# Where the matmuls' operands lie in on-chip memory: activations and split weights first, in a two-layer transformer trunk

## The chip, the cores and the metric

One core of a Trainium2 chip runs the whole program in one launch. The metric is the device time of one execution in microseconds (us); lower is better. Three executions of the kernel before took 2267.03 to 2269.26 us, with a median of 2267.74 us.

## What is computed

The input x has 256 tokens of 2048 float32 features. Two layers follow, with all products in float32 accuracy:

```python
# layer 0
hn = rmsnorm(h, attn_norm_g[0])
h  = h + diff_attention(hn, w_qkv, ...) @ w_o_a        # 8 heads, two softmax maps each, T5 bias
h  = h + square(relu(rmsnorm(h, mlp_norm_g[0]) @ w_in[0])) @ w_out[0]     # 2048 -> 8192 -> 2048
# shared keys, values, forget gates from rmsnorm(h, kv_norm_g): w_k, w_v, w_f
# layer 1
h  = h + forgetting_attention(rmsnorm(h, attn_norm_g[1]) @ w_q, k, v, c) @ w_o_b    # 16 heads
h  = h + square(relu(rmsnorm(h, mlp_norm_g[1]) @ w_in[1])) @ w_out[1]
out = rmsnorm(h, final_norm_g)
```

All weight matrices together are about 400 MB, and each number of them is read from DRAM once.

## The kernel before, in words

**The stream of weights.** Every weight matrix is cut into granules of 128 partitions x 1024 float32 numbers (512 KB). `load` (L161) brings one into a tile `raw` (4 buffers) from SyncE's DMA queue. `split` (L169, the copy in L171 on ScalarE) writes its high part `whi` in the matmul's rounded format float32r, and `split_low` (L173, L174 on VectorE) writes the remainder `wlo` = raw - whi. Both have 5 buffers, and up to 4 granules are split ahead of the products. Activations are held in the same manner: a tile of 128 x 2 x 512 numbers holds, for two blocks of 128 features, the high parts of 256 tokens and then their low parts. A product of float32 accuracy is then hi.hi + hi.lo + lo.hi.

**Two forms of unit.** TensorE holds one operand, the stationary one of 128 x 128, and streams the other, the moving one, through it.

- A token-major unit (kind B, `mm_b`, L185 to L187) makes 256 tokens x 512 columns. The *activation* is stationary, and the split *weights* move, 512 columns at a time: 3 matmuls for each of 2 token blocks and 16 row blocks, 96 in a unit of 2048 rows.
- A feature-major unit (kind A, `mm_a`, L200 and L203) makes 256 features x 256 tokens. The *weights* are stationary, and the activation moves: 512 columns (high and low parts) with whi in L200, and 256 columns with wlo in L203, 32 of each in a unit.

**Which activation tiles a unit reads.** Tiles `x0` to `x7` hold the normed residual stream (for the attention's and the MLP's first products and the shared keys and values). Tiles `hx0` to `hx7` hold the MLP's hidden activations, eight at a time, in layer 0 before that the attention's outputs, and in layer 1 the query operand. The four tiles `oT` hold the attention's outputs of layer 1. So:

| product | form | stationary | moving | units |
|---|---|---|---|---|
| values of both layers | B | x | whi, wlo | 8 |
| w_o_a | B | hx | whi, wlo | 4 |
| w_out of both MLPs | B | hx | whi, wlo | 32 |
| w_o_b | B | oT | whi, wlo | 12, of 24 or 48 matmuls, 384 in all |
| queries and keys of layer 0, keys of layer 1, w_in of both MLPs | A | whi, wlo | x | 88 |
| queries of layer 1 | A | whi, wlo | hx | 8 |

**The order of the work.** It is written out by hand: a list of slots, one granule of one unit each, and tables `pre`, `mid` and `post` that place the side work (softmax, norms, transposes, evacuations of results) before, amid and after a slot. Nothing is reordered by a scheduler.

**Where a tile lies.** All tiles in on-chip memory come from one pool. A tag takes its place in a partition when its first tile is made, behind the tags that came before it, with all its buffers, in steps of 32 bytes. The places in the kernel before, in bytes from the start of a partition:

| tiles | bytes each | before, from | to | after, from | to |
|---|---|---|---|---|---|
| x0 to x7 | 4096 | 38592 | 71360 | 1152 | 33920 |
| hx0 to hx7 | 4096 | 177568 | 210336 | 33920 | 66688 |
| oT x4 (hT too) | 4096 | 210336 | 226720 | 66688 | 83072 |
| whi x5 | 4096 | 89792 | 110272 | 83072 | 103552 |
| wlo x5 | 4096 | 110272 | 130752 | 103552 | 124032 |
| ident, tri, upto, h0 to h3, z1, zs, ssb, osb, wfs, gains | 384 to 4096 | 1152 | 38592 | 124032 | 161472 |
| raw x4, junk | 4096, 2048 | 71360 | 89792 | 161472 | 179904 |
| e, v, T/NC/gf, R, q, k, aT and small ones | up to 8192 | 130752 | 177568 | 179904 | 226720 |

Of the kernel before, what the change touches and what calls it, by code (L numbers as in the profile page):

```python
# [12 lines left out]
F32R = mybir.dt.float32r  # L13
# [5 lines left out]
DRAM = bass.MemoryType.DRAM  # L19

P = 128
D = 2048
S = 256
HD = 128
FF = 8192
NA = 8          # differential heads
NF = 16         # forgetting heads
CW = 512        # columns of a token-major unit
NCH = D // CW
# [4 lines left out]
SCALE = HD ** -0.5  # L34
NREL = 383      # rel = -255 .. 127

LA = 4          # granules split ahead of the products
NRAW = 4        # granules in flight from DRAM
NSPL = LA + 1


@with_exitstack
def kernel(ctx: ExitStack, tc: tile.TileContext, *args):
# [10 lines left out]

    # ------------------------------------------------------------------ constants
    ident = sb.tile([P, P], F32, tag="ident", name="ident")
# [7 lines left out]

    # 1 where a token is up to another: within a block of 128, and a block before
    upto = sb.tile([P, S], F32, tag="upto", name="upto")
# [4 lines left out]

    # residual stream, token-major, by chunks of 512 features
    h = [sb.tile([P, 2, CW], F32, tag=f"h{c}", name=f"h{c}") for c in range(NCH)]

# [3 lines left out]

    # the activation engine's tables come in beside the first loads
    warm = sb.tile([P, 1], F32, tag="warm", name="warm")  # L80
    nc.vector.memset(warm, 0.0)
    nc.scalar.activation(out=warm, in_=warm, func=AF.Exp)
    # gains as columns: rows of 128 features, transposed
    grow = [sb.tile([n, P], F32, tag="z1", bufs=2, name="grow") for n in (32, 50)]
# [36 lines left out]

    # ------------------------------------------------------------------ the stream of weights
    # side work by slot of the tensor engine: before its weights' split, amid it, and after the products
    pre, mid, post = (defaultdict(list) for _ in range(3))
    order = []      # (unit, granule, token tiles): what the tensor engine does

    class Gran:
        """Weights of one transfer: kk tiles of 128 rows, 1024 numbers a partition."""

# [3 lines left out]
    class Unit:  # L133
        """One result in two banks: its granules, its operand, and what takes it."""

# [9 lines left out]
    def unit_b(W, r0, nk, c0, xs, done):  # L145
        """[256, 512] = x . W[r0 : r0 + nk * 128, c0 : c0 + 512], token-major."""
        gs = []
        for k in range(0, nk, 2):
            src = W[r0 + k * P:r0 + (k + 2) * P, c0:c0 + CW].rearrange("(k p) c -> p k c", p=P)
            gs.append(Gran(src, 2))  # L150
        return Unit("B", gs, xs, done)

    def unit_a(W, c0, xs, done):
        """[256 features, 256 tokens] = (x . W[:, c0 : c0 + 256]) transposed."""
        gs = []
        for k in range(0, 16, 4):
            src = W[k * P:(k + 4) * P, c0:c0 + 256].rearrange("(k p) c -> p k c", p=P)
            gs.append(Gran(src, 4))
        return Unit("A", gs, xs, done)
# [51 lines left out]

    # ------------------------------------------------------------------ pieces
    def new_x(tag):
        """Two 128-row tiles of an operand: high parts of 256 tokens, then low parts."""
        return sb.tile([P, 2, 2 * S], F32R, tag=tag, name=tag)

    def turn(c, tps):
        """h[c] feature-major, into two banks."""
        for b in range(2):
            for j in range(2):  # L220
                for m in range(2):
                    f = (2 * b + j) * P
                    nc.tensor.transpose(tps[b][:, (j * 2 + m) * P:(j * 2 + m + 1) * P],  # L223
                                        h[c][:, m, f:f + P], ident)

    def split_turned(c, tps, gain, dst, bs=(0, 1)):
        """High and low parts of gain . h[c] turned, from two pieces of 512 columns."""
        at = [(b, j, 4 * c + 2 * b + j) for b in bs for j in range(2)]
# [17 lines left out]
    def rsqrt(ssum, n, scale, eps, name, bufs=1):  # L246
        """(ssum * scale + eps) ** -0.5 by columns: three Newton steps from the exponent's half."""
        v = sb.tile([P, n], F32, tag="rs_v", bufs=2, name="rs_v")
# [18 lines left out]
    class Norm:  # L267
        """Row statistics of the residual stream: rstd by token, and along the free axis."""

# [32 lines left out]
    def pair_sum(u):  # L302
        """The two halves of a feature-major unit's banks added: [128, 2, 256]."""
        z1 = sb.tile([P, 2, S], F32, tag="z1", bufs=2, name="z1")
# [14 lines left out]

    # ------------------------------------------------------------------ prologue: x, T5 bias, lambda  # L320
    XT = {}
# [16 lines left out]
    def bias_in():  # L338
        T = sb.tile([P, NA, S], F32, tag="tnc", bufs=2, name="T")
        # T[q, head, j] = F[head, q, 127 - q + j]: rows of 383, read 382 apart  # L340
        src = bias["F"].rearrange("h q r -> h (q r)")[:, 127:127 + P * (NREL - 1)]
# [5 lines left out]
    def build_lambda():  # L347
# [6 lines left out]
        nl = sb.tile([P, 1], F32, tag="nlam", name="nlam")  # L354
        # -(e1 - e2 + init)
        nc.vector.tensor_tensor(out=nl, in0=ex[:, 1:2], in1=ex[:, 0:1], op=ALU.subtract)
        nc.vector.tensor_scalar(out=nl, in0=nl, scalar1=-LAMBDA_INIT, scalar2=None, op0=ALU.add)
        bias["nlam"] = nl

    # ------------------------------------------------------------------ layer 0: differential attention  # L360
    vt = {}
# [139 lines left out]

    # boundary after the last product that a chunk of h takes
    def h_done(c, norm, gain, key, with_scale=False):
# [33 lines left out]

    n_mlp0, n_att1, n_mlp1 = (Norm.__new__(Norm) for _ in range(3))      # started by their first chunk

# [8 lines left out]
    def wo(W, kind, p0, p1, dones):  # L548
        """h += o . W over the head pairs p0 to p1; the last pair of the first two chunks comes last."""
        us = [unit_b(W[0], p0 * S, 2 * (p1 - p0), c * CW,  # L550
# [11 lines left out]

    # ------------------------------------------------------------------ squared-ReLU MLP
    HX = {}

    def mlp(l, norm, key, last, start=None):
        for q in range(4):
# [20 lines left out]
            for c in range(NCH):  # L588
                u = unit_b(w_out[l], q * D, 16, c * CW, lambda hk=hk: HX[hk], adds[c] if q < 3 else last[c])
                if l == 1 and q == 3 and c == NCH - 1:  # L590
                    # the last result: one token tile ends before the other
                    u.apart = True
# [6 lines left out]

    # ------------------------------------------------------------------ layer 1: forgetting attention  # L600
    fg = {}

    def gates(s0):
# [24 lines left out]
        def gate1():  # L628
            # z = logits by token; n = min(z, 0); t = exp(-|z|)
            zc = sb.tile([P, 2, 2 * NF], F32, tag="fg_zc", name="fg_zc")  # L630
# [14 lines left out]
        def gate2():  # L645
            # log1p(t) = 2 atanh(s), s = t / (2 + t) in [0, 1/3]
            t = fg["t"]
# [19 lines left out]
        def gate4():  # L667
            # log sigmoid = min(z, 0) - log1p(exp(-|z|))
            p = fg["p"]
# [5 lines left out]
        def sums():  # L675
            # over the tokens up to each: by head and token
            t = ps.tile([P, 512], F32, tag="sc", name="cs")
# [40 lines left out]
    def spread_c(g):  # L718
        """-c over the keys on every partition, causal on the diagonal blocks: diagonal 0 | full | diagonal 1."""
        t = sb.tile([P, 4, 3 * P], F32, tag="tnc", bufs=2, name="NC")  # L720
# [8 lines left out]
    def fox_pair(g, i):  # L729
        """Heads 4 g + 2 i and the next."""  # L730
        st = {}
# [87 lines left out]
    def v_first(s0):  # L819
        """Beside the first unit of layer 1: the forget gates, and the query operand."""  # L820
        gates(s0 + 4)
        xq_plan(s0)
# [10 lines left out]
    def qkv_f(g):  # L833
# [6 lines left out]
        for i in range(2):  # L840
# [3 lines left out]
            def then(e, plan=plan, i=i):  # L844
                # the last values come after the last queries
                plan(e, e + 7 if g < 3 else e + 17 - 7 * i)
# [14 lines left out]

    # ------------------------------------------------------------------ last MLP and the final norm
    fin = {}
# [43 lines left out]

    # ------------------------------------------------------------------ emission
    grs, at = [], []        # the granules as they come; how many the slots so far have taken
    for u, i, ms in order:  # L910
# [20 lines left out]
    load_x(2)  # L931
    # the tensor engine's clock comes up while the first rows are on their way
    busy = sb.tile([P, CW], F32, tag="junk", name="busy")
# [41 lines left out]
    for s in range(n + 2):  # L975
        for f in pre.pop(s, []):
            f()
        # while x comes in, one granule less is split ahead
        upto_g = min(ng, at[s] + (LA if s >= 8 else LA - 1)) if s < n else ng
# [31 lines left out]
def bucket_onehot():  # L1011
    """Row b, column r: 1 where the T5 bucket of rel = r - 255 is b."""
    rel = np.arange(-255, NREL - 255)
# [29 lines left out]
```

## Time and profile before

| | |
|---|---|
| median of three executions | 2267.74 us (2267.03 to 2269.26) |
| span of the profiled execution, first to last instruction | 2266.5 us |
| what lies around that span in the timed executions, median less span | 1.2 us |
| instructions | 28986 |
| TensorE, matmuls busy | 2234.6 us, 99% of the span |
| TensorE, weight loads busy (beside the matmuls) | 1874.0 us, 83% |
| VectorE busy | 1356.8 us, 60% |
| ScalarE busy | 1022.4 us, 45% |
| DMA | 416.06 MB, mean 184 GB/s |

How to read it: consecutive matmuls overlap in time, since each one's record reaches from its start to the modelled end of its pipeline. So "99% busy" says that TensorE hardly ever waits; it doesn't say how much time a matmul costs. What a matmul costs is the distance from its start to the start of the next one, called its step below, and it is read from a stretch of known length in which a known number of matmuls start.

### The profile page before, as it was taken

The numbers are of one execution on the slowest core, as the hardware profiler recorded it, in microseconds if no ns is written. First come the engines' busy times: TensorE is split into PE (matmuls) and PEld (weight loads), VectorE is DVE, ScalarE is ACT, GpSimd is POOL, SyncE is SP. The second block draws the span as 40 slices with busy tenths as digits, with TensorE's granted clock in tenths as the row PEclk, the third lists the DMA queues.
The fourth block names the chain that finished last, engine by engine and source line by source line (L and its number), as shares of the span: only waits on it lengthen the run. The fifth ranks groups of instructions, "written<-read, shape, count | busy, mean of one in ns | idle before, by whom it ended". The sixth has DMA issues, their size and how long they took to land.

```text
span 2266.5 us, 28986 instructions
## 1 busy us (share of the span) xinstructions
PE 2234.6 (99%) x11272; PEld 1874.0 (83%) x11272; DVE 1356.8 (60%) x1768; ACT 1022.4 (45%) x1343; POOL 14.0 (1%) x19
## 2 busy tenths in 40 slices
PE   8799999999999999999999999999999999999998
PEld 6688888888888888888888888888888888888886
DVE  4566665665565565466576556656645655655655
ACT  4454554443444344344554444454434434433443
POOL 0000000000000000000001000000000000000000
PEclk9899999999999999999999999999999999999999
DMA  7655555556556655666556565556565565565563
GB/s 198 200 178 176 159 176 177 171 187 200 180 187 194 191 184 188 187 189 188 170 169 203 175 192 181 178 168 203 186 187 185 186 194 178 186 197 178 187 200 130
DMA packets 319332, 416.06 MB, mean 184 GB/s; under 512 B 15066, under 2 KB 218972, under 8 KB 319068
## 3 DMA queue, kind: packets, MB, share of 16 engines
q1 hardware_dynamic: 319148, 414.20, 58.4%
q8 instruction: 88, 1.44, 0.3%
q14 instruction: 48, 0.39, 0.1%
q10 hardware_dynamic: 48, 0.02, 0.0%
HBM read 410.49 MB, written 3.68 MB: 183 GB/s over the span
## 4 chain that ended last, share of the span: by engine, by line
PE 97%; DMA 2%; DVE 0%; ACT 0%; issue 0%; SPq 0%; DVEq 0%; ACTq 0%
PE acc L200 31%; PE acc L203 16%; PE acc L187 15%; PE acc L185 15%; PE acc L186 15%; DMA raw<-in_w_qkv_a 2%; PE tp L223 1%; PE sc L396 0%; PE sc L739 0%; PE sc L187 0%; PE sc L186 0%; PE sc L185 0%; PE o L797 0%; PE fp L610 0%; PE o L798 0%; PE tpo L474 0%
## 5 line engine op out<-in xcount | busy, mean ns | idle before, releaser
L174 DVE TENSOR_TENSOR wlo<-raw,whi 128x1024 fp32r<-128x1024 f32 x767 | 926.1, 1224 | 646.9 <-ACT whi L171 646.1
L171 ACT CAST whi<-raw 128x1024 fp32r<-128x1024 f32 x767 | 797.3, 1050 | 751.5 <-PE acc L187 460.2
L200 PE MATMUL acc<-x,whi 128*128 128x512 f32 x2816 | 993.8, 399 | 18.7 <-ACT whi L171 18.7
L203 PE MATMUL acc<-x,wlo 128*128 128x256 f32 x2816 | 776.9, 281 | 0.5 <-DVE wlo L174 0.5
L200 PEld LDWEIGHTS acc<-x,whi 128*128 128x128 f32 x2816 | 525.5, 188 | 139.4 <-ACT whi L171 19.0
L203 PEld LDWEIGHTS acc<-x,wlo 128*128 128x128 f32 x2816 | 532.7, 189 | 9.1 <-DVE wlo L174 1.0
L185 PE MATMUL acc<-whi,hx 128*128 128x512 f32 x1120 | 443.4, 396 | 0.0
L187 PE MATMUL acc<-whi,hx 128*128 128x512 f32 x1120 | 442.4, 395 | 0.0
L186 PE MATMUL acc<-wlo,hx 128*128 128x512 f32 x1120 | 442.3, 395 | 0.0
L187 PEld LDWEIGHTS acc<-whi,hx 128*128 128x128 f32 x1120 | 209.9, 187 | 51.3
L186 PEld LDWEIGHTS acc<-wlo,hx 128*128 128x128 f32 x1120 | 210.0, 187 | 51.0
L185 PEld LDWEIGHTS acc<-whi,hx 128*128 128x128 f32 x1120 | 210.0, 187 | 50.5
L307 DVE TENSOR_TENSOR zs<-acc,z 128x512 f32<-128x512 f32 x96 | 66.3, 691 | 102.8 <-ACT z L306 102.8
L306 ACT COPY z<-acc 128x512 f32<-128x512 f32 x96 | 56.4, 587 | 157.1 <-PE acc L200 157.1
L581 ACT CAST hx<-s 128x512 fp32r<-128x512 f32 x64 | 39.8, 622 | 143.2 <-DVE s L579 143.2
L185 PE MATMUL acc<-whi,x 128*128 128x512 f32 x256 | 102.7, 401 | 0.2 <-ACT x L230 0.2
L187 PE MATMUL acc<-whi,x 128*128 128x512 f32 x256 | 100.1, 391 | 0.6 <-DVE x L233 0.6
L186 PE MATMUL acc<-wlo,x 128*128 128x512 f32 x256 | 99.8, 390 | 0.0
L200 PE MATMUL acc<-hx,whi 128*128 128x512 f32 x256 | 92.1, 400 | 0.0
L582 DVE TENSOR_TENSOR hx<-s,hx 128x512 fp32r<-128x512 f32 x64 | 44.3, 693 | 44.0 <-ACT hx L581 44.0
L203 PE MATMUL acc<-hx,wlo 128*128 128x256 f32 x256 | 70.6, 281 | 0.0
L318 DVE TENSOR_TENSOR h<-acc,h 128x512 f32<-128x512 f32 x88 | 56.7, 686 | 17.9 <-PE acc L187 17.8
(172 smaller groups left out, 1170.0 us busy)
## 6 DMA issues: line engine op xcount, KB each, us to landing
raw<-in_w_mlp_in SPq DMA_DIRECT2D x256, 512.0 KB, 3.9
raw<-in_w_mlp_out SPq DMA_DIRECT2D x256, 512.0 KB, 3.8
raw<-in_w_qkv_a SPq DMA_DIRECT2D x96, 512.0 KB, 4.6
raw<-in_w_o_a SPq DMA_DIRECT2D x32, 512.0 KB, 4.2
raw<-in_w_v_b SPq DMA_DIRECT2D x32, 512.0 KB, 3.8
raw<-in_w_k_b SPq DMA_DIRECT2D x32, 512.0 KB, 3.7
raw<-in_w_q_b SPq DMA_DIRECT2D x32, 512.0 KB, 3.8
raw<-in_w_o_b SPq DMA_DIRECT2D x32, 512.0 KB, 3.6
```

Of the source, the lines that this page charges most:

```text
L171: nc.scalar.copy(out=g.hi, in_=g.raw)
L174: nc.vector.tensor_tensor(out=g.lo, in0=g.raw, in1=g.hi, op=ALU.subtract)
L185: nc.tensor.matmul(bank[m], xh, hi[:, j, :], start=k == 0, stop=False)
L186: nc.tensor.matmul(bank[m], xh, lo[:, j, :], start=False, stop=False)
L187: nc.tensor.matmul(bank[m], xl, hi[:, j, :], start=False, stop=k == nk - 1)
L200: nc.tensor.matmul(bank[n], hi[:, j, w], xt, start=k == 0, stop=k == 15)
L203: nc.tensor.matmul(bank[n][:, 0:S], lo[:, j, w], xt[:, 0:S], start=False, stop=False)
L306: nc.scalar.copy(out=z1, in_=u.acc[:, :, S:2 * S])
L307: nc.vector.tensor_tensor(out=zs, in0=u.acc[:, :, 0:S], in1=z1, op=ALU.add)
L318: nc.vector.tensor_tensor(out=h[c][:, m, :], in0=u.bank[m], in1=h[c][:, m, :], op=ALU.add)
L581: nc.scalar.copy(out=t[:, :, 0:S], in_=s)
L582: nc.vector.tensor_tensor(out=t[:, :, S:2 * S], in0=s, in1=t[:, :, 0:S], op=ALU.subtract)
```

## The change

Ahead of everything else in the kernel, one tile of each tag is made for x0 to x7, hx0 to hx7, and as many tiles as there are buffers for oT (4), whi (5) and wlo (5). Nothing reads or writes these first tiles; their tags take their places in the pool, and the tiles that the program makes later under these tags get the same places. All other tags follow behind. Comments and docstrings are taken out as well, which moves line numbers alone.

```diff
     ctx.enter_context(tc.manual_schedule())
 
+    for tag in [f"x{i}" for i in range(8)] + [f"hx{i}" for i in range(8)]:
+        sb.tile([P, 2, 2 * S], F32R, tag=tag, name=tag)
+    for _ in range(4):
+        sb.tile([P, 2, 2 * S], F32R, tag="oT", bufs=4, name="oT")
+    for tag in ("whi", "wlo"):
+        for _ in range(NSPL):
+            sb.tile([P, 1024], F32R, tag=tag, bufs=NSPL, name=tag)
+
     ident = sb.tile([P, P], F32, tag="ident", name="ident")
```

The instructions of every engine, their order, what each waits for and the shapes that they work on are the same in both programs, 17469 entries in each. What differs are the addresses of tiles, as in the table above. Against the starts of lines of 64 bytes, x, whi and wlo start at a multiple of 64 before, and hx and oT at an odd multiple of 32; after the change all five start at multiples of 128. The other tiles moved by multiples of 4096 bytes.

## Rows read from the trace of the kernel before

**Rows 1.** The page: engines' busy time, granted clock by slices, and the ending chain.
```profile
PE 2234.6 (99%) x11272; PEld 1874.0 (83%) x11272; DVE 1356.8 (60%) x1768; ACT 1022.4 (45%) x1343; POOL 14.0 (1%) x19
...
PEclk9899999999999999999999999999999999999999
...
PE 97%; DMA 2%; DVE 0%; ACT 0%; issue 0%; SPq 0%; DVEq 0%; ACTq 0%
PE acc L200 31%; PE acc L203 16%; PE acc L187 15%; PE acc L185 15%; PE acc L186 15%; DMA raw<-in_w_qkv_a 2%; PE tp L223 1%; PE sc L396 0%; PE sc L739 0%; PE sc L187 0%; PE sc L186 0%; PE sc L185 0%; PE o L797 0%; PE fp L610 0%; PE o L798 0%; PE tpo L474 0%
```

**Rows 2.** TensorE's waits: waiter, releaser, us in total, times, longest.
```profile
PE acc L200 <- ACT whi L171: 18.7, 1, 18.7
PE up L937 <- DVE busy L934: 1.6, 1, 1.6
```

**Rows 3.** Five single units: w_out; values, keys, queries of layer 1; w_in.
```profile
core 0: us, PE busy (x) PEld busy (x) DVE busy (x) ACT busy (x) POOL busy (x), PEclk, DMA share, GB/s
535.45:557.84 22.39, 22.39 (x97) 17.99 (x96) 11.00 (x10) 8.39 (x8) 0.00 (x0) 1.00 0.58 188
1320.43:1342.18 21.75, 21.75 (x97) 18.02 (x96) 11.19 (x11) 8.44 (x8) 0.00 (x0) 1.00 0.63 194
1342.19:1353.49 11.30, 11.30 (x66) 9.81 (x65) 4.90 (x4) 5.35 (x6) 0.00 (x0) 1.00 0.57 182
1353.49:1364.78 11.29, 11.29 (x66) 9.81 (x65) 6.20 (x6) 4.67 (x5) 0.00 (x0) 1.00 0.60 189
602.66:613.96 11.30, 11.30 (x66) 9.88 (x65) 6.10 (x6) 4.23 (x5) 0.00 (x0) 1.00 0.61 188
```

**Rows 4.** Line L185's matmuls by tiles: count, duration ns min/median/max, first and last start.
```profile
L185 PE MATMUL acc<-whi,hx x1120: 392/396/582, 325.6 to 2234.0; 128*128 128x512 f32 x187
...
L185 PE MATMUL acc<-whi,x x256: 387/389/586, 7.1 to 1486.5; 128*128 128x512 f32 x128
...
L185 PE MATMUL acc<-whi,oT x128: 393/396/580, 1294.8 to 1536.5; 128*128 128x512 f32 x128
...
L185 PE MATMUL sc<-whi,hx x32: 393/395/397, 2234.7 to 2256.4; 128*128 128x512 f32 x32
```

**Rows 5.** Line L200's matmuls by tiles, the same columns.
```profile
L200 PE MATMUL acc<-x,whi x2816: 387/396/796, 34.4 to 2167.2; 128*128 128x512 f32 x188
...
L200 PE MATMUL acc<-hx,whi x256: 389/395/503, 1182.7 to 1463.2; 128*128 128x512 f32 x128
```

**Rows 6.** The stretches of four w_out units and of eight w_in units, columns as in rows 3.
```profile
513.07:602.66 89.59, 89.59 (x386) 71.96 (x385) 45.44 (x42) 34.59 (x34) 0.00 (x0) 1.00 0.61 191
602.66:692.67 90.01, 90.01 (x514) 78.34 (x513) 58.53 (x62) 40.71 (x46) 0.00 (x0) 1.00 0.58 183
```

**Rows 7.** Groups of instructions, shapes apart: count, busy us, mean ns, idle before them.
```profile
L174 DVE TENSOR_TENSOR wlo<-raw,whi 128x1024 fp32r<-128x1024 f32 x767 | 926.1, 1224 | 646.9 <-ACT whi L171 646.1 <-PE sc L396 0.7
L171 ACT CAST whi<-raw 128x1024 fp32r<-128x1024 f32 x767 | 797.3, 1050 | 751.5 <-PE acc L187 460.2 <-PE acc L200 194.1 <-issue 37.3
...
L307 DVE TENSOR_TENSOR zs<-acc,z 128x512 f32<-128x512 f32 x96 | 66.3, 691 | 102.8 <-ACT z L306 102.8
...
L306 ACT COPY z<-acc 128x512 f32<-128x512 f32 x96 | 56.4, 587 | 157.1 <-PE acc L200 157.1
...
L313 DVE TENSOR_TENSOR k<-zs,R 128x512 f32<-128x512 f32 x16 | 11.1, 693 | 0.5
...
L803 ACT CAST oT<-o 128x512 fp32r<-128x512 f32 x8 | 4.7, 588 | 20.2 <-PE o L798 20.2
L525 ACT COPY hT<-tp 128x512 f32<-128x512 f32 x8 | 4.7, 587 | 1.6 <-DVE x L233 1.6
```

**Rows 8.** DMA issues by line: count, KB each, median us from issue to landing.
```profile
raw<-in_w_mlp_in SPq DMA_DIRECT2D x256, 512.0 KB, 3.9
...
gf<-in_final_norm_g SPq DMA_DIRECT2D x1, 1024.0 KB, 6.8
```

## The prediction, made before the result was known

> **What bounds the kernel now.** I began with the busy times and the chain of waits on the page: matmuls are in flight for 99% of the span, 97% of the chain that ended last is TensorE, and nearly all of that is the five matmul lines L185, L186, L187, L200 and L203, at a granted clock of 90% or more in all slices but the second [rows 1]. Next came TensorE's own waits, to see whether those 97% hide a late operand. They don't: one wait of 18.7 us near the start and one of 1.6 us are all of note [rows 2]. So the time is the number of matmuls times the step of each, and an edit can only pay or cost by changing the step, or by making a split so late that TensorE waits again.
>
> The edit adds no instruction and moves none; it changes addresses. So the question for the trace is whether the step depends on where an operand lies, and the kernel before holds an experiment on that: token-major units that are equal in everything but the place of their stationary tile. The table of stretches has a w_out unit (stationary hx, from byte 177568 up) and a unit of values (stationary x, bytes 38592 to 71360). Each has 96 matmuls of 512 columns; the records counted are 97, since the last matmul of the unit before is still in flight. Both run at clock 1.00 with the same 8 casts beside them, and the one with more DMA traffic is the shorter. They take 22.39 and 21.75 us [rows 3]: 233.2 and 226.6 ns a step. That this is no accident of two units is seen in the durations by tile: the median L185 matmul takes 389 ns with x, and 396 ns both with hx and with oT (bytes 210336 up) [rows 4]. The same 7 ns that lengthen the step lengthen the record.
>
> Feature-major units tell about the moving operand. One with x moving and one with hx moving stand side by side in layer 1: 11.30 and 11.29 us, and a w_in unit takes 11.30 us too [rows 3]. The medians of L200 are 396 and 395 ns [rows 5]. So where the moving activation lies has cost nothing up to now; where the stationary activation lies has.
>
> **The change part by part.**
>
> *The stationary activations of the token-major units move down.* hx goes from 177568 to 33920, which is nearly where x was, and whi and wlo move down by only 6720 bytes, so that the pair hx and whi comes to lie as x and whi lay. Two properties could make hx slow before: its height in the partition, or its start at an odd multiple of 32 bytes where x starts at a multiple of 64. The trace of before can't part them, since hx and oT have both and x has neither. I needn't choose: after the change hx has neither, in the one sense and in the other. So the w_out unit becomes like the unit of values, 22.39 - 21.75 = 0.64 us shorter. How many such units: L185 has 1120 + 32 matmuls with hx and 128 with oT, 1280 in all, and L186 and L187 have as many each, so 3840 matmuls or 40 units of 96 [rows 4]. 40 x 0.64 = **25.6 us**. All of it lies on the path that sets the end, since TensorE doesn't wait in these units: four of them in a row take 89.59 us, 22.40 each [rows 6]. What the oT tiles give (4 of the 40 units, 2.6 us) is a little less sure, as they come to lie above all x tiles of before (66688 to 83072).
>
> *x moves from 38592 down to 1152.* As stationary operand of the 8 value units it was in the fast case already. No matmul in float32r has had its activation so low, so the step there isn't shown. By the nearest rows: at worst it becomes 233.2 ns, as for hx, and costs 8 x 0.64 = 5.1 us; at best it gains as much again. I take 0, being nearest to the x rows.
>
> *The feature-major units*: x moves away from under the weights, and whi and wlo now start at multiples of 128 bytes. Rows 3 say that 140,000 bytes more or less for the moving tile are worth 0.01 us in a unit, so I take 0. The ends: if each of the 3072 L200 matmuls gained the 6.7 ns that place was worth in the other form, 20.6 us less; if the 2816 with x lost as much, 18.9 us more.
>
> *All other buffers move up.* raw goes from 71360 to 161472, so the two split instructions read from higher bytes, and h, z1, zs and the scratch tiles follow. What height costs VectorE and ScalarE: a ScalarE copy of 128x512 from the accumulator takes 587 ns into z1 at 19616, and 587 and 588 ns into hT and oT above 210336; a VectorE sum takes 691 ns into zs at 23712 and a product 693 ns into k above 167008 [rows 7]. So 0 to 2 ns an instruction. Even that is hidden: before the casts ScalarE sat idle for 751.5 us in total, and before the subtractions VectorE for 646.9 us [rows 7]. If this cover were gone, 767 subtractions at 2 ns would be 1.5 us. The loads: 512 KB land in 3.9 us, and a transfer of 1024 KB into a tile at 152576 took 6.8 us [rows 8], less than twice as long; a granule is consumed every 2.8 us with four in flight, so there are some 7 us of cover.
>
> *What is late next.* In the faster units a granule is consumed every 21.75 / 8 = 2.72 us. The unit of values ran at exactly that pace without a wait, with ScalarE busy for 8.44 and VectorE for 11.19 of 21.75 us and the DMA engines at 0.63 [rows 3]. So the stream of weights keeps up and nothing is late next.
>
> The sum: 2266.5 - 25.6 = 2240.9 us for the span, and with the 1.2 us by which the median stands above the profiled span, **2242 us**.
>
> A page bears on the first term. Rows 3 show equal units 0.64 us apart by the place of the stationary tile. The page "TensorE: Matmul & The Clock Gate" of the Trainium skill, in "Step-by-step: what each phase is for", gives the weight load a read port of its own and says that loading the next tile doesn't steal bandwidth from the running matmul, with a time set by its columns alone; its "Back-to-back issue gap" makes the step N/2.4 + 2.5 ns, about 216 ns here, wherever operands lie. By that page the first term is 0 and the time stays at 2267.7 us. The trace disagrees with it already in the kernel before, at 233.2 and 226.6 ns.
>
> **The rivals.**
>
> 1. *Place isn't the cause, no change: 2267.7 us.* The hx units could be slower for what the tiles hold, or for something in how those units follow each other. For it: the two kinds of tile differ in content too. Against it: hx holds attention outputs in w_o_a and squared activations in w_out, oT a third kind, and all have the same 396 ns [rows 4]. It is also what the rule of separate ports in the Trainium skill, cited above, would give.
>
> 2. *The feature-major units gain as well: about 2221 us.* If what costs is a conflict between the reads of both operands, or the alignment to lines beyond 64 bytes, L200 gets 6.7 ns too: 2242 - 20.6. For it: a pair of L200 and L203 there takes 11.30 / 32 = 353 ns, 126 ns over the step of one 512-column matmul in the values' unit, where 256 columns at that rate would take 113, so there is something to gain. Against it: 11.30 and 11.29 us with two quite different places of x and hx [rows 3].
>
> 3. *The lowest bytes are no good place for a moving tile: about 2261 us.* x is the moving tile of 2816 L200 matmuls; 6.7 ns each give back 18.9 of the 25.6 us.
>
> 4. *Slower: the split falls behind, 2338 us.* raw now lies higher, and both split engines read it. Were reads up there slow, VectorE would be first: over eight w_in units it is busy for 58.53 of 90.01 us [rows 6], so it has 3.9 us to spare in a unit, about 1 us for each of the four subtractions. The rival decides once L174 takes over 2.2 us in place of 1.224; doubled to 2.45 us, it would make each of 96 feature-major units about 1 us longer, 2242 + 96 = 2338. Against it stand the 691 and 693 ns above. TensorE would then show waits on wlo again.
>
> **How the numbers follow.** The forecast has 0.69; its own range is 2237 (x gains too) to 2247 us (x loses 5.1, or oT gives nothing). Rival 2 has 0.13, rival 1 has 0.10, rivals 3 and 4 have 0.04 each. The range takes in the forecast and rival 2, which is 0.82: 2220 to 2250 us. A measurement of this kernel can tell about 0.2%, 4.5 us, from no change. Faster by more than that are the forecast and rivals 2 and 3: 0.86. The same: rival 1, 0.10. Slower: rival 4, 0.04.
>
> **What would show it.** In the changed kernel's trace, a w_out unit should take 21.75 us in place of 22.39, and the medians of L185's successor should be 389 ns with hx and with oT as with x; the four units of one MLP quarter should take 87.0 us in place of 89.6. Eight w_in units should stay at 90.0 us. The splits should stay at 1050 and 1224 ns within 3 ns, and TensorE's waits should remain the one at the start. If w_out units stay at 22.4 us, place is not the cause; if w_in units get shorter, rival 2 is at work, and if they get longer, rival 3; waits of TensorE on wlo would be rival 4.

## The result, and the profile after

The changed kernel takes **2244.43 us** (median of four executions, 2244.32 to 2244.77) against 2268.43 us for the kernel before (four, 2267.03 to 2269.26). The ratio on record, estimated from all of these executions, is 0.9897, with an interval of 0.9883 to 0.9911. The profiled span fell from 2266.5 to 2242.7 us, by 23.8 us. The three new loops move the rest of the code down by nine lines, so L185, L186, L187, L200 and L203 are L194, L195, L196, L209 and L212 now, and the splits L171 and L174 are L180 and L183.

The page of the changed kernel, where the busy times, the chain that ended last and the two splits answer to [rows 1, 7]:

```profile
PE 2213.4 (99%) x11272; PEld 1877.7 (84%) x11272; DVE 1356.7 (60%) x1768; ACT 1020.8 (46%) x1343; POOL 13.6 (1%) x19
...
PE 97%; DMA 2%; DVE 0%; ACT 0%; issue 0%; SPq 0%; DVEq 0%; ACTq 0%
PE acc L209 32%; PE acc L212 16%; PE acc L194 15%; PE acc L196 15%; PE acc L195 15%; DMA raw<-in_w_qkv_a 2%; PE tp L232 1%; PE sc L405 0%; PE sc L748 0%; PE sc L194 0%; PE sc L195 0%; PE sc L196 0%; PE o L806 0%; DMA h<-in_x 0%; PE fp L619 0%; PE o L807 0%
...
L183 DVE TENSOR_TENSOR wlo<-raw,whi 128x1024 fp32r<-128x1024 f32 x767 | 926.1, 1225 | 627.4 <-ACT whi L180 626.8
L180 ACT CAST whi<-raw 128x1024 fp32r<-128x1024 f32 x767 | 795.9, 1048 | 730.5 <-PE acc L196 443.5
...
raw<-in_w_mlp_in SPq DMA_DIRECT2D x256, 512.0 KB, 4.0
```

The shape of the profile is the old one: TensorE in flight for 99% of the span and making 97% of the chain. Its busy time fell by 21.2 us, while the splits moved by 1 and 2 ns and the granules land in 4.0 us instead of 3.9. TensorE's waits are still the one near the start and little else; waiter, releaser, us in total, times and longest:

```profile
PE acc L209 <- ACT whi L180: 17.5, 1, 17.5
PE up L946 <- DVE busy L943: 1.6, 1, 1.6
```

The matmuls of L194 and L209 by tiles (columns as in [rows 4]; the weight loads between the lines are left out):

```profile
L194 PE MATMUL acc<-whi,hx x1120: 387/389/586, 324.3 to 2210.9; 128*128 128x512 f32 x187
...
L194 PE MATMUL acc<-whi,x x256: 387/389/775, 7.0 to 1472.7; 128*128 128x512 f32 x128
...
L194 PE MATMUL acc<-whi,oT x128: 387/389/585, 1282.3 to 1521.6; 128*128 128x512 f32 x128
```

```profile
L209 PE MATMUL acc<-x,whi x2816: 387/398/796, 34.6 to 2146.0; 128*128 128x512 f32 x188
...
L209 PE MATMUL acc<-hx,whi x256: 387/395/500, 1170.4 to 1449.3; 128*128 128x512 f32 x128
```

The median of L194 with hx and with oT fell from 396 to 389 ns, to what x had and kept; L209 stayed within 2 ns. And the same units of the program as in [rows 3, 6], by stretches: w_out, values, one w_in, four w_out, eight w_in (columns as there):

```profile
531.47:553.22 21.75, 21.75 (x97) 18.02 (x96) 11.01 (x10) 8.38 (x8) 0.00 (x0) 1.00 0.63 196
1307.39:1329.15 21.76, 21.76 (x97) 18.02 (x96) 11.21 (x11) 8.39 (x8) 0.00 (x0) 1.00 0.61 194
...
596.75:608.04 11.29, 11.29 (x65) 9.81 (x64) 6.10 (x6) 4.20 (x4) 0.00 (x0) 1.00 0.62 191
509.69:596.74 87.05, 87.05 (x385) 72.06 (x384) 45.42 (x42) 34.54 (x34) 0.00 (x0) 1.00 0.64 197
596.75:687.14 90.39, 90.39 (x513) 78.48 (x512) 58.56 (x62) 40.63 (x46) 0.00 (x0) 1.00 0.58 182
```

A w_out unit has become a unit of values: 22.39 to 21.75 us, a step of 226.6 ns. For the whole program I summed the steps of each kind in both traces, matmul by matmul, since their order is the same. After less before, in us: token-major with hx -22.34 (3456 steps), with oT -2.24 (384), with x +0.20 (768); feature-major with x +1.09, with hx -0.46; all else 0. Together -23.75, which is the span's 23.8.

### The profile page after: what moved, and what is told of

It reads as the page before. It is cut to its first block, busy times and chain, and to the rows that moved or that the text cites. A ratio compares the mean times of both kernels' runs of the same rounds, so it can differ in the third digit from the quotient of the medians.

```text
span 2242.7 us, 28986 instructions
## 1 busy us (share of the span) xinstructions
PE 2213.4 (99%) x11272; PEld 1877.7 (84%) x11272; DVE 1356.7 (60%) x1768; ACT 1020.8 (46%) x1343; POOL 13.6 (1%) x19
## 4 chain that ended last, share of the span: by engine, by line
PE 97%; DMA 2%; DVE 0%; ACT 0%; issue 0%; SPq 0%; DVEq 0%; ACTq 0%
PE acc L209 32%; PE acc L212 16%; PE acc L194 15%; PE acc L196 15%; PE acc L195 15%; DMA raw<-in_w_qkv_a 2%; PE tp L232 1%; PE sc L405 0%; PE sc L748 0%; PE sc L194 0%; PE sc L195 0%; PE sc L196 0%; PE o L806 0%; DMA h<-in_x 0%; PE fp L619 0%; PE o L807 0%
## 5 line engine op out<-in xcount | busy, mean ns | idle before, releaser
L183 DVE TENSOR_TENSOR wlo<-raw,whi 128x1024 fp32r<-128x1024 f32 x767 | 926.1, 1225 | 627.4 <-ACT whi L180 626.8
L180 ACT CAST whi<-raw 128x1024 fp32r<-128x1024 f32 x767 | 795.9, 1048 | 730.5 <-PE acc L196 443.5
L209 PE MATMUL acc<-x,whi 128*128 128x512 f32 x2816 | 996.1, 399 | 17.5 <-ACT whi L180 17.5
L212 PE MATMUL acc<-x,wlo 128*128 128x256 f32 x2816 | 777.7, 281 | 0.5 <-DVE wlo L183 0.5
L209 PEld LDWEIGHTS acc<-x,whi 128*128 128x128 f32 x2816 | 525.7, 188 | 139.6 <-ACT whi L180 17.8
L212 PEld LDWEIGHTS acc<-x,wlo 128*128 128x128 f32 x2816 | 532.9, 189 | 9.2 <-DVE wlo L183 1.0
L194 PE MATMUL acc<-whi,hx 128*128 128x512 f32 x1120 | 436.9, 390 | 0.0
L196 PE MATMUL acc<-whi,hx 128*128 128x512 f32 x1120 | 436.0, 389 | 0.0
L195 PE MATMUL acc<-wlo,hx 128*128 128x512 f32 x1120 | 435.8, 389 | 0.0
L196 PEld LDWEIGHTS acc<-whi,hx 128*128 128x128 f32 x1120 | 210.2, 188 | 43.8
L195 PEld LDWEIGHTS acc<-wlo,hx 128*128 128x128 f32 x1120 | 210.3, 188 | 43.5
L194 PEld LDWEIGHTS acc<-whi,hx 128*128 128x128 f32 x1120 | 210.3, 188 | 43.1
L194 PE MATMUL acc<-whi,x 128*128 128x512 f32 x256 | 103.4, 404 | 0.0
L195 PE MATMUL acc<-wlo,x 128*128 128x512 f32 x256 | 100.5, 393 | 0.0
L196 PE MATMUL acc<-whi,x 128*128 128x512 f32 x256 | 100.5, 392 | 0.0
L209 PE MATMUL acc<-hx,whi 128*128 128x512 f32 x256 | 91.6, 398 | 0.0
L212 PE MATMUL acc<-hx,wlo 128*128 128x256 f32 x256 | 70.5, 281 | 0.0
```

Of the source, the lines that this page charges most:

```text
L180: nc.scalar.copy(out=g.hi, in_=g.raw)
L183: nc.vector.tensor_tensor(out=g.lo, in0=g.raw, in1=g.hi, op=ALU.subtract)
L194: nc.tensor.matmul(bank[m], xh, hi[:, j, :], start=k == 0, stop=False)
L195: nc.tensor.matmul(bank[m], xh, lo[:, j, :], start=False, stop=False)
L196: nc.tensor.matmul(bank[m], xl, hi[:, j, :], start=False, stop=k == nk - 1)
L209: nc.tensor.matmul(bank[n], hi[:, j, w], xt, start=k == 0, stop=k == 15)
```

## The experiments

Why were hx and oT slow? The prediction left two properties open, and I added a third:

- **Height**: a stationary tile high in the partition is slow.
- **Alignment**: a stationary tile that starts at an odd multiple of 32 bytes is slow.
- **Distance**: what counts is the number of bytes from the stationary tile's start to the moving tile's. Within a unit the slices of the activation lie 512, 1024 and 2048 bytes apart and those of the weights 2048, and the distances from whi and from wlo differ by multiples of 4096, so a tile has one distance modulo 512 and longer periods can't be told apart here. Before, from x to whi it is 89792 - 38592 = 51200, which is 0 modulo 512; from hx it is -87776 and from oT -120544, both 288. After, all three are 0.

### Four placements that part the theories

`low_odd`: the changed kernel with 32 bytes ahead of hx0 and 32 more ahead of whi. hx and oT are low and start at odd multiples of 32; distance 32 for hx and oT, 64 for x.

```diff
+    sb.tile([P, 8], F32, tag="pad1", name="pad1")   # ahead of hx0
...
+    sb.tile([P, 8], F32, tag="pad2", name="pad2")   # ahead of whi
```

> The operands stay in the lowest part, but hx and oT start at odd multiples of 32 bytes again (33952 and 66720); x, whi and wlo stay at multiples of 64. Height theory (bytes far up are slow): w_out units stay at 21.75 us, 2244 us in all. Alignment theory (a stationary tile that starts off a multiple of 64 bytes costs 6.7 ns a matmul): w_out units 22.4 us, about 2269 us. Offset theory (what counts is the distance between stationary and moving tile, which has to be a multiple of 64): also 22.4 us and 2269 us.

Measured: 2271.04 us (2269.74 to 2271.21), ratio to the kernel before 1.0011 (1.0002 to 1.002). The whole gain is gone. Stretches of w_out and values:

```profile
535.14:557.54 22.40, 22.40 (x97) 17.99 (x96) 10.99 (x10) 8.39 (x8) 0.00 (x0) 1.00 0.61 189
1321.40:1343.79 22.39, 22.39 (x97) 18.14 (x96) 11.18 (x11) 8.38 (x8) 0.00 (x0) 1.00 0.59 188
```

hx lies at 33952 and is as slow as it was at 177568, so height falls. That this unit of values, with an aligned stationary x at 1152, is slow as well speaks against alignment already. It is one of eight, though, and the only one in which no other matmul falls in between: the seven others step at 229.0 to 229.3 ns on average, where this one takes 233.3. So x at a distance of 64 shows two levels within one kernel.

`high_even`: the kernel *before*, with 32 bytes ahead of hx0 and nothing else. hx and oT stay high and start at multiples of 64; distance 256.

```diff
+            if hd == 0:
+                sb.tile([P, 8], F32, tag="pad", name="pad")
```

> The kernel before with 32 bytes left free ahead of hx0, so that hx and oT stay high (177600 and 210368 up) but start at multiples of 64. Height theory: as before, w_out units 22.4 us, 2268 us. Alignment theory: w_out units 21.75 us, about 2244 us. Offset theory: 2244 us as well if a multiple of 64 is enough, 2268 us if it takes the multiples of 2048 that x and whi have in both kernels.

Measured: 2245.46 us (2244.89 to 2245.55), ratio 0.9898 (0.9883 to 0.9913). The stretch of w_out:

```profile
532.51:554.27 21.76, 21.76 (x97) 18.02 (x96) 10.99 (x10) 8.44 (x8) 0.00 (x0) 1.00 0.62 196
```

One gap of 32 bytes does as much as the whole change, to within about 1 us. Moving the five groups to the bottom of the memory was not what brought the gain.

`w_odd`: the changed kernel with 32 bytes ahead of whi and 32 behind wlo. x, hx and oT stay at multiples of 128, whi and wlo start at odd multiples of 32; distance 32 for all three.

```diff
+    sb.tile([P, 8], F32, tag="pad2", name="pad2")   # ahead of whi
...
+    sb.tile([P, 8], F32, tag="pad3", name="pad3")   # behind wlo
```

> The changed layout, but whi and wlo start at odd multiples of 32 bytes; x, hx and oT at multiples of 64. Here the weights are moving in the token-major units and stationary in the feature-major ones. Height theory: 2244 us. Alignment theory: token-major units stay at 21.75 us, feature-major units get longer by 6.7 ns for each of 64 matmuls, 11.3 to 11.7 us, about 2285 us in all (2265 if only the 32 matmuls of 512 columns pay). Offset theory: both forms pay, token-major 22.4 us, 2290 us or more.

Measured: 2271.45 us (2270.74 to 2273.28), ratio 1.0014 (1.0005 to 1.0024). w_out, values and eight w_in units:

```profile
534.95:557.35 22.40, 22.40 (x97) 17.99 (x96) 11.00 (x10) 8.38 (x8) 0.00 (x0) 1.00 0.60 188
1321.27:1343.66 22.39, 22.39 (x97) 17.99 (x96) 11.18 (x11) 8.39 (x8) 0.00 (x0) 1.00 0.60 188
...
602.15:692.26 90.11, 90.11 (x513) 78.42 (x512) 58.53 (x62) 40.60 (x46) 0.00 (x0) 1.00 0.57 183
```

Well-aligned stationary tiles are slow once the moving tile is displaced. In the feature-major units, where whi and wlo are the *stationary* tiles and now lie at odd multiples of 32, nothing is lost (90.11 against 90.39 us). Alignment of the stationary tile falls. The distance theory, as I had written it down, missed here too: it said that both forms pay, 2290 us or more. Only the token-major form does.

`all_odd`: the changed kernel with all five groups displaced by the same 32 bytes. Everything starts at an odd multiple of 32; all distances 0.

```diff
+    sb.tile([P, 8], F32, tag="pad0", name="pad0")   # ahead of x0
...
+    sb.tile([P, 8], F32, tag="pad3", name="pad3")   # behind wlo
```

> The changed layout shifted by 32 bytes as a whole: x, hx, oT, whi and wlo all start at odd multiples of 32, and their distances from each other are those of the changed kernel. Height theory and offset theory: 2244 us, nothing changes. Alignment theory: token-major units 22.4 us, now the units of values too, and feature-major units up to 11.7 us: 2290 to 2315 us.

Measured: 2243.16 us (2242.99 to 2243.39), ratio 0.9889 (0.9872 to 0.9905):

```profile
529.58:551.34 21.76, 21.76 (x97) 18.02 (x96) 11.00 (x10) 8.40 (x8) 0.00 (x0) 1.00 0.63 193
1305.74:1327.50 21.76, 21.76 (x98) 18.02 (x96) 11.19 (x11) 8.40 (x8) 0.00 (x0) 1.00 0.61 193
```

Distance says this and alignment doesn't; height says it too, but is out since `low_odd` and `high_even`. With `w_odd` this run makes the cleanest pair: in the built programs every tile lies at the same bytes in both, but for x, hx and oT (and hT, in the place of oT), which lie 32 bytes higher in `all_odd`. Those 32 bytes between activations and weights are the whole difference of 28 us, 2271.45 and 2243.16.

### Is it the parity, or the distance itself?

After these four, a rule that is simpler than a distance would still do: "both tiles must have the same remainder against 64 (or 128)". Two placements test it: a gap between oT and whi of 64 bytes (`all_64`) and of 128 bytes (`all_128`), so that x, hx and oT all have that distance. With 128 every one of the five groups starts at a multiple of 128.

```diff
+    sb.tile([P, 16], F32, tag="gap", name="gap")   # 32 in place of 16 for 128 bytes
```

> The changed kernel with 64 bytes left free ahead of whi, so that x, hx and oT all lie at distance 64 from the weights, and every tile still starts at a multiple of 64. At this distance the x units showed 229.6 ns a step in one run, and hx7 alone 233.3 ns in another. Offset theory with the distance as the only cause: hx, oT and x show one step here, and the token-major part costs 40 to 48 units x 0.28 us (229.6 ns, about 2257 us) or x 0.64 us (233.3 ns, about 2273 us). Alignment to 64 as the cause: 226.7 ns and 2244 us.

> The same with 128 bytes left free, so that all tiles start at multiples of 128 and lie at distance 128. A single hx tile at 128 showed 232.1 ns. Offset theory: 232 to 233 ns in all token-major units, about 2268 us. Alignment to 64 or 128 as the cause: 226.7 ns and 2244 us.

Measured: 2254.73 us for 64 bytes (2254.1 to 2254.84; ratio 0.9939, 0.9916 to 0.9961), 2266.89 us for 128 (2266.35 to 2268.36; ratio 0.9997, 0.9985 to 1.0008). w_out and values with 64 bytes:

```profile
533.03:555.00 21.97, 21.97 (x98) 18.03 (x96) 11.00 (x10) 8.41 (x8) 0.00 (x0) 1.00 0.62 190
1312.59:1334.55 21.96, 21.96 (x97) 18.02 (x96) 11.19 (x11) 8.39 (x8) 0.00 (x0) 1.00 0.61 190
```

and with 128 bytes, where the third row is the eight w_in units:

```profile
534.79:557.18 22.39, 22.39 (x97) 18.01 (x96) 11.00 (x10) 8.42 (x8) 0.00 (x0) 1.00 0.60 188
1319.45:1341.76 22.31, 22.31 (x97) 18.09 (x96) 11.20 (x11) 8.40 (x8) 0.00 (x0) 1.00 0.61 189
...
601.98:691.82 89.84, 89.84 (x513) 78.71 (x512) 58.55 (x62) 40.68 (x46) 0.00 (x0) 1.00 0.58 185
```

Steps of 228.8 and 233.2 ns: tiles that share every alignment up to 128 bytes are as slow as before. Parity falls too; the distance itself counts. The pair of rows at a distance of 64 also shows that it is not the only thing: the unit of values takes 21.96 us here and 22.39 in `low_odd`, at the same distance. There it follows a unit with oT at a distance of 32, which is slow; here one with oT at 64. In the built programs nothing but hx, oT and hT lies elsewhere, by 32 bytes, and in `low_odd` itself the other seven units of values step at some 229 ns, as they do here. So the step depends on what ran just before as well.

### Which distances are good

Four more kernels give each tile a place of its own; they keep three raw buffers in place of four, which pays for the room, and their total times say nothing of the change.

`scan`: 32 bytes between the hx tiles, and whi and wlo displaced by their own amounts in each buffer. It was a poor design: whi and wlo of one granule mostly have different distances, so that the steps mix.

```diff
+HI_AT = (0, 4, 0, 12, 2)
+LO_AT = (0, 0, 8, 4, 6)
...
+        sb.tile([P, 8], F32, tag=f"gap{i}", name=f"gap{i}")   # behind each hx tile
```

> One kernel that holds many distances between stationary and moving tile: the hx tiles lie 4096 + 32 bytes apart, the buffers of whi and wlo 4096 + 64, and within its buffer a split weight starts 0 to 48 bytes in, by the buffer's number; three raw buffers make room for it. It is a measuring device, not a version. If the distance modulo some power of two sets the step of a token-major matmul, all pairs of tiles with one distance show one step, about 227 ns at multiples of 128, 230 at odd multiples of 64, 233 at odd multiples of 32, and the starts themselves don't matter. If it is a collision of two reads that some distance avoids, other distances (16, 48, 96 bytes) may lie below 226 ns. If 227 ns is the floor for other reasons, no distance does.

Measured: 2273.34 us; the means of its granules with hx lie mostly between 230 and 235 ns a step, and the distances explain little of that. Inconclusive, but for one thing: none came as low as the 226.7 ns of distance 0; the lowest was 229.4.

`scan2`: weights at one place, each x and hx tile displaced by its own number of bytes (4 per number).

```diff
+X_AT = (0, 1, 2, 3, 5, 6, 9, 17)
+HX_AT = (0, 4, 8, 12, 16, 20, 24, 28)
```

> The measuring device made cleaner: whi and wlo all at distance 0 from each other modulo 512, and hx0 to hx7 set 0, 16, 32, 48, 64, 80, 96 and 112 bytes off that (modulo 128); x0 to x7 set 0, 4, 8, 12, 20, 24, 36 and 68 bytes off. In a granule of a token-major unit the distance is now one and the same for 12 matmuls. Offset theory: the step of a granule goes by its hx tile, 226.7 ns at 0, about 230 at 64, 233 at 32 and 96, in all units alike. If the collision of two reads is avoidable, one of 16, 48, 80 or 112 lies below 226 ns. Rival (only whether a distance is a multiple of 128 matters): 226.7 at 0 and one single higher level elsewhere.

A granule is multiplied with one tile, so a w_out unit now holds eight different distances, 12 matmuls each. The first five granules of one unit, with hx0 to hx4 at 0, 368, 224, 80 and 448 (columns as in [rows 3]):

```profile
545.94:548.67 2.73, 2.73 (x14) 2.25 (x12) 2.42 (x3) 1.05 (x1) 0.00 (x0) 1.00 0.61 209
548.67:551.39 2.72, 2.72 (x13) 2.25 (x12) 1.23 (x1) 1.05 (x1) 0.00 (x0) 1.00 0.63 201
551.39:554.19 2.80, 2.80 (x14) 2.25 (x12) 1.23 (x1) 1.05 (x1) 0.00 (x0) 1.00 0.60 210
554.19:556.95 2.76, 2.76 (x14) 2.25 (x12) 1.22 (x1) 1.05 (x1) 0.00 (x0) 1.00 0.58 183
556.95:559.75 2.80, 2.80 (x14) 2.26 (x13) 1.23 (x1) 1.05 (x1) 0.00 (x0) 1.00 0.61 194
```

2.72 us is 226.7 ns a step and 2.80 is 233.3: within one unit the speed changes from granule to granule with the place of the tile.

`scan4`: other distances in the same manner, by a gap of 128 bytes ahead of x, one of 384 ahead of hx, and these displacements of hx:

```diff
+HX_AT = (16, 0, 0, 0, 24, 16, 16, 16)
```

> The cleaner device once more, with other distances from the weights down to the stationary tiles, modulo 512: hx0 to hx7 at 448, 384, 256, 128, 416, 320, 192 and 64, and all x tiles at 384. Offset theory with a period of 256 or less: 256 and 0 alike at 226.7 ns, 448 like 192, 384 like 128, 320 like 64. With a period of 512: 128 differs from 384, 64 from 448. The feature-major pairs with x, all at 384 now, stay within 1% of the 352.8 ns that they take at 0 if the distance doesn't matter in that form.

Mean steps of both, counted from start to start, of the third to the eleventh matmul of each granule (some 320 uninterrupted steps for each hx tile, 72 for each x tile, about 570 for the x of `scan4`):

| distance mod 512, hx | ns | distance mod 512, hx | ns | distance mod 512, x | ns |
|---|---|---|---|---|---|
| 0 | 227.5 | 256 | 227.4 | 60 | 233.2 |
| 16 | 228.1 | 304 | 233.2 | 116 | 233.3 |
| 64 | 233.3 | 320 | 228.9 | 220 | 234.3 |
| 80 | 229.9 | 368 | 226.8 | 248 | 230.5 |
| 128 | 232.1 | 384 | 233.0 | 360 | 231.1 |
| 160 | 234.0 | 416 | 234.3 | 380 | 226.7 |
| 192 | 233.3 | 448 | 233.1 and 233.5 | 384 | 232.5 |
| 224 | 233.4 | | | 492 | 233.3 |

The good ones are 0, 256 and, unexpectedly, 368 and 380; most are slow, and some lie between. One tile is left out of the table: x0 of `scan2`, at distance 0 like hx0, steps at 229.5 ns. It holds the first granule of its units, and most of these follow a unit of the other form; in the one that follows oT at distance 0 without a pause it takes 226.7. Distances that lie 256 apart show nearly the same step (0 and 256, 128 and 384, 160 and 416, 192 and 448), and 320 shows what 64 showed in `all_64`; so the period may be 256 bytes and not 512. But 64 itself is at 233.3 here, and no one rule reads all rows.

`scan3`: x and hx fixed, the weights displaced by buffer.

```diff
+W_AT = (92, 36, 96, 32, 28)
```

> The same device with the weights displaced in place of the activations: all activation tiles at distance 0 from each other modulo 512, and the five buffers of whi and wlo 368, 16, 128, 256 and 112 bytes above that, so that a granule has one distance in both forms of unit. Offset theory for the token-major units: 226.7 ns at 368 and 256, about 228 at 16, whichever of the two tiles was displaced; 128 and 112 are new. Feature-major units: in the run before, pairs of L200 and L203 in a unit with hx moving took 346 to 347 ns at 368 and at 16 against 350 elsewhere; if the distance does that, x units show it as well, some 5 ns a pair under the 352.8 ns that they take at 0. If it came from the neighbours in time, all buffers show 352 to 353 ns.

Measured: 2264.93 us. The buffers came up in another order than I had counted on, so the distances are not those of the expectation, and 16, 128, 256 and 112 weren't tested. Two of the five kinds of granule got different distances for whi and wlo and can't be read. The others, with hx and counted as in the table: 227.2 ns at 0, 233.3 at 144, 231.1 at 368. The first agrees with the table, and 144 is as slow as its neighbours there; 368 was at 226.8 in `scan2`, among other neighbours, so what ran before matters here too.

Feature-major pairs (L209 and L212 together) took 349 to 350 ns in `scan3` at 0 and 368 (counted from the stationary to the moving tile, as above) and 353 at 144, alike with x and with hx moving. So place shows in this form too, at about 1%, and in `scan2` at more: the pairs that read x6 and x7, displaced by 36 and 68 bytes, took 358.2 and 361.3 ns on average, where the changed kernel has 352.1 and 353.9.

### A version that beats both

The feature-major units are most of what is left. Their pair of a 512-column and a 256-column matmul takes 11.29 / 32 = 353 ns, and in the whole trace 235.4 of that, on average, lies between the start of a matmul with whi and that of the one with wlo. `grouped` is the changed kernel with the matmuls of a granule in another order: eight with whi, then eight with wlo (in the last granule of a unit the other way round).

```diff
-        for j in range(g.kk):
-            for n in range(2):
-                whole()
-                part()
+        for f in (part, whole) if k0 + g.kk == 16 else (whole, part):
+            for j in range(g.kk):
+                for n in range(2):
+                    f(j, n)
```

> The changed kernel with the feature-major matmuls of a granule in another order: its eight with whi, then its eight with wlo (in the last granule of a unit the other way round), in place of pairs. In the changed kernel a pair takes 236 + 117 ns from start to start, and where two of one kind follow each other, at the ends of units and in the last row block, steps were 231 and 119 ns. Theory that the step goes by which matmul follows: a granule becomes 7 x 231 + 236 + 7 x 119 + 117 = 2803 in place of 2824 ns, 8 us over 384 granules, about 2236 us. Rival (the load of the next weights sets the pace of these units whatever the order): no change, 2244 us, or more, since the short matmuls then stand in a row with nothing to cover a weight load.

Measured: **2231.76 us** (2231.25 to 2232.91), ratio to the kernel before 0.9839 (0.9823 to 0.9856), so some 12 us below the changed kernel. Stretches of one w_in unit, four w_out and eight w_in:

```profile
595.22:606.37 11.15, 11.15 (x65) 9.84 (x64) 6.09 (x6) 4.20 (x4) 0.00 (x0) 1.00 0.66 196
508.18:595.21 87.03, 87.03 (x385) 72.07 (x384) 45.41 (x42) 34.54 (x34) 0.00 (x0) 1.00 0.64 197
595.22:684.44 89.22, 89.22 (x513) 78.69 (x512) 58.54 (x62) 39.91 (x46) 0.00 (x0) 1.00 0.58 185
```

Eight w_in units are 90.39 - 89.22 = 1.17 us shorter; times 12, for all 96 feature-major units, that would be 14.0 us. Summed step by step they gave 11.7, so the others gained less, and the span fell by 11.6. A long matmul that follows a long one now starts 229.6 ns after it, a short one after a long one 226.8 instead of 235.4, a short one after a short one 119.6. The token-major units are what they were.

The expectation had left the step from long to short at 236 ns, so the time came out 4 us below its 2236: a step goes by more than the matmul that follows. Grouping also changes which accumulation bank follows which, but that isn't it: in the last row blocks of the changed kernel 96 steps from long to short go over to the other bank and take 235.5 ns on average, as do those that stay in one bank (235.4). Why the grouped order is faster isn't shown.

## Why the prediction was right, and where it was not

**The bound.** TensorE's step by the number of matmuls, with no wait behind it [rows 1, 2]: right. The profile after has the same shape, and the 23.8 us are all in steps.

**The first term, 25.6 us.** It measured 24.6 (22.34 with hx, 2.24 with oT): 0.62 us a unit where I took 0.64. The stretches of w_out gained 6.6 ns a step, as forecast; w_o_a and the units of an MLP in which TensorE has other work in between gained 4.5 to 6.4. The oT tiles, of which I was less sure, gave 2.24 of 2.6 us.

**The reason behind it was wrong.** The step reads "Two properties could make hx slow before: its height in the partition, or its start at an odd multiple of 32 bytes", and "I needn't choose: after the change hx has neither". It is neither: `low_odd` is slow at a low place, `high_even` is fast at the old height, `w_odd` is slow with well-aligned stationary tiles and `all_odd` fast with none aligned. What counts is the distance between the two tiles that a matmul reads. The sum held because of a half-sentence that stood beside the two properties, that "the pair hx and whi comes to lie as x and whi lay": a distance of 0 modulo 512 in both cases. It stood there as nearness (whi and wlo move by only 6720 bytes), not as a distance that has to be a certain one, so for the cause the right number was luck: the tiles' sizes are multiples of 512, and laid side by side they come to a distance of 0. Had the change put the same tiles just as low with 32 or 128 bytes more between oT and whi, the prediction would have been the same 2242 us, and the time 2271 or 2267.

**x down to 1152, taken as 0**: +0.20 us. x keeps distance 0. The bound of 5.1 us was the right price for the bad case: in `w_odd`, where x gets distance 32, its steps sum to 3.9 us more than before.

**Feature-major, taken as 0**: +0.63 us (1.09 with x, -0.46 with hx), eight w_in units 90.39 in place of 90.01 us. Small, as [rows 3, 5] said; rivals 2 and 3, with 20.6 less and 18.9 more, are out. Place isn't quite without effect here: eight units take 89.84 us in `all_128` and 90.39 at distance 0, and over all 96 units the steps of `all_128` sum to 5.1 us less than those of the changed kernel.

**All other buffers, taken as 0**: splits 1048 and 1225 ns, granules landing in 4.0 us, no wait on wlo to speak of. Rival 4 is out, and the cover was not touched.

**Rival 1**, that place isn't the cause, is out by 32 bytes (`high_even`). No mean token-major step here came below 226 ns, and it went up to 234 by place alone. "TensorE: Matmul & The Clock Gate" of the Trainium skill, section "Back-to-back issue gap", gives N/2.4 + 2.5 ns, about 216 ns for 512 columns, for a matmul by itself, and some 131 ns a matmul of 512 columns for a stream of weight loads and matmuls. The prediction went by the first alone, though its units are such a stream. The runs agree with neither figure, and the measurement decides.

**2242 against 2244.4**: 1.0 us from the first term, 0.6 from the feature-major units and 0.2 from x make the span 2242.7 where I had 2240.9. The last 0.6 us are the step from span to median: I took 1.2 us from three executions of the kernel before, and the changed kernel's profiled execution has 2244.49 - 2242.7 = 1.8.

**What stays open.** Why a distance is good or bad isn't shown. The mean record of a weight load with hx was 187 ns before and is 188 now, so the load itself doesn't get shorter; that a load and the stream beside it hinder each other in reading the memory is argued, not shown. Open too are why 64 and 368 show two levels, by what period the pattern repeats (256 bytes, 512 or more), and why the feature-major form, with the same two kinds of tile in exchanged roles, lost little or nothing at the distances that cost the token-major form 6.6 ns a step.

## What to carry to other kernels

Look for units that do equal work and compare their times: a difference of 3% in a step without any wait is a question to the addresses, and a gap of 32 bytes, which an allocator leaves or doesn't leave by chance, answers it in one run. Where TensorE is the bound, choose the places of the two tiles that a matmul reads *together* (here 0 modulo 512 between them was good, and 256 as well), and read the distance off the built program; a tile's own height, or its alignment to 64 or 128 bytes, gave nothing here. A single unit isn't enough to judge a distance, since the step can depend on what ran before. And where long and short matmuls alternate, try them in groups.

## What the runs showed that I had not expected

- 32 bytes of empty space are worth 22.8 us (2268.23 to 2245.46), 1.0% of this kernel.
- All five groups at odd multiples of 32 bytes are as fast as at multiples of 128: 2243.16 and 2244.43 us.
- Some distances that look arbitrary, 368 and 380, reached the lowest step, some 226.7 ns, in one kernel (368 was at 231.1 in another); 384, four bytes on from 380, was at 232.5.
- The same distance can show two levels by what ran before it: 64 bytes gave 21.96 and 22.39 us for the same unit.
- The order of long and short matmuls, at unchanged work, is worth some 12 us.
